# Carried HGRN states loaded ahead into weight buffers, prompt-state stores moved behind the weight loads, and another order of the mixer's projection units

## The chip, the cores and the metric

The kernel runs on one core of a Trainium2 chip. The metric is device time in microseconds for one execution, inputs and outputs in HBM. Before is given by three runs, and the profiled execution is a further one.

## The reference, cut to what matters

One step of a decoder trunk of two layers (width 1024) over 256 prompt rows and 32 sample rows (8 sequences of 4 tokens with carried state). Each layer is a half-step FFN, a mixer and a second half-step FFN, with a layer norm after each:

```
x <- LN(alpha*x + 0.5*SwiGLU_1(x))
z  = x @ W_in            # mix_w_in, 1024 x 3584
o  = concat[RWKV-7 (4 heads of 64), HGRN2 (4 heads of 128), chunk-gMLP (4 of 64)] @ W_out   # mix_w_out
x <- LN(alpha*x + o)
x <- LN(alpha*x + 0.5*SwiGLU_2(x))
```

HGRN2 is a gated linear recurrence. For a sample sequence the output of a head is the query times the carried state (128 x 128, one for each of 8 sequences and 4 heads, 2 MB a layer) plus products within the four new tokens, and the new state is the old one times the total decay plus keys times values. The prompt starts from a zero state. The chunk-gMLP normalises its v half, mixes it over 128 positions, and multiplies by its u half. Everything is float32. Outputs are the trunk's rows, all final states, and the normalised v rows of the samples (`cm_v_sample`).

## The kernel before, in words

All activations stay in SBUF with the features on partitions and the 288 rows along the free dimension. A dense product is done in blocks of at most 512 x 256 weights. `prep` (L338) loads a block on SP's queue into a `raw` buffer (3 of them); ACT rounds it into `wh` and DVE writes the rest into `wl` (3 buffers each), and TensorE makes three products per 128 x 128 piece (`d<-x,wl`, `d<-x,wh` twice), 24 a block. The mixer's input projection for the HGRN and chunk-gMLP parts is made in ten units of 256 columns straight from `raw` in float32 (`d<-ax,raw`, 16 products a unit). `ORDER` (L1798) lists these units: f, q, v, o are forget gate, query, value and output gate of the HGRN (two units each), cv and cu the two halves of the gMLP.

The mixer of a layer is written as generators, one per piece of work (`CHAINS`), which `go` in `mix` (L1695) advances in turn between the units. `hg_scan` builds the HGRN decay products, `hg_mix` makes the prompt's HGRN output, `hg_sample` (L1497) the samples' output and `hg_states` the samples' new states, `cm_mix` (L1624) the gMLP, `rw_prompt` and its fellows the RWKV part. A scheduler of the language then places the instructions on the engines by priorities; each engine executes its list strictly in that order. So an instruction that must wait holds back all that stands behind it on its engine, DMA issues included: SP's list holds nearly all of them.

Names that matter below. `hs` are the four tiles of carried HGRN states of a layer (one a head, 512 KB); `hqm` the masked queries; `hp` their 32 products with the states on TensorE; `hs<-hs,hgP` on POOL the decay of a state, which overwrites the tile that `hp` reads; `hvb` the masked values, `hn` their product with the keys, `hs<-hs,hn` on DVE the sum that is stored as the new state. `cvn` is the gMLP's v and `cst` its statistics, `cO`/`cOs` the mix over positions on TensorE, `cM` its result times u. `hO`, `hS`, `hon`, `hot`, `ho` are the prompt's HGRN output on its way to the layout of `mix_w_out`'s input, `OM`, `gst`, `pgt`, `OT` the same for RWKV, and `x` the split input of `mix_w_out`. That dense product starts with four blocks for output columns 0 to 511 (96 products), whose first group of rows is features 0, 1, 6, 7: RWKV's two and the gMLP's two. PSUM has four banks (`pm`) for all small products.

In the kernel before, the states are loaded in `hg_sample` into tiles of the general pool `m4` (19 buffers), the prompt's new states are stored at the end of `rw_prompt` and `hg_mix`, and all these DMAs stand on SP's queue among the loads of `mix_w_out`.

Of the kernel before, what the change touches and what calls it, by code (L numbers as in the profile page):

```python
# [8 lines left out]
F32 = mybir.dt.float32  # L9
# [11 lines left out]
NS = 32  # L21
# [17 lines left out]
class Trunk:  # L39
# [298 lines left out]
    def prep(self, spec):  # L338

        name, l, ks, n0, pool = spec  # L340
        nk = len(ks)
        nc = self.nc
        raw = self.wp.tile([128, 4, 256], F32, tag="raw", name=f"raw{nc.next_id()}", bufs=B["raw"])
        runs = [i for i in range(nk + 1) if i in (0, nk) or ks[i] != ks[i - 1] + 1]
        for a, b in zip(runs, runs[1:]):
            src = self.I[name][l][ks[a] * 128:(ks[b - 1] + 1) * 128, n0:n0 + 256]
            nc.sync.dma_start(raw[:, a:b], src.rearrange("(c p) n -> p c n", p=128))
        if pool == "raw":
            return raw
        hi = self.wp.tile([128, 4, 256], F32R, tag="wh", name=f"wh{nc.next_id()}", bufs=B["wh"])  # L350
        lo = self.wp.tile([128, 4, 256], F32R, tag="wl", name=f"wl{nc.next_id()}", bufs=B["wl"])
        with self.prio("prep"):
            self.act(hi[:, :nk], raw[:, :nk])
            self.sub(lo[:, :nk], raw[:, :nk], hi[:, :nk].bitcast(F32), nc.gpsimd if pool else None)
        return hi, lo
# [581 lines left out]
    def rw_prompt(self, l, KR, bh, kh, V, eP, em):  # L937

        nc, O = self.nc, self.O
# [191 lines left out]
        for c in range(2):  # L1131
            self.tr(p[0:64, c * 128:(c + 1) * 128], S[:, c, 3])
        so = self.ep.tile([64, 256], F32, tag="rwSo", name=f"rwSo{l}", bufs=1)
        nc.vector.tensor_copy(so, p[0:64, 0:256])
        nc.sync.dma_start(O["rwkv_state_prompt"][l, 0].rearrange("g v k -> v g k"),
                          so.rearrange("p (g k) -> p g k", g=4))

    def rw_load(self, l):
        nc, I = self.nc, self.I
# [307 lines left out]
    def hg_mix(self, l):  # L1447
# [15 lines left out]
        for j in range(2):  # L1463
# [20 lines left out]
                for h in range(4):  # L1484
                    self.stt(SP[:, h], SP[:, h], P[:, 256 * h + 255:256 * h + 256], p[:, h], ALU.mult, ALU.add)
            yield
        nc.sync.dma_start(O["hgrn_state_prompt"][l, 0].rearrange("h k v -> k h v"), SP)

    def hrms(self, nm, sq, n):
        nc = self.nc  # L1490
        r = self.ep.tile([128, 4], F32, tag="hrm", name=f"hrm{nm}", bufs=2)[:, 0:n]
        nc.vector.tensor_reduce(r, sq, axis=AX.X, op=ALU.add)
        self.act(r, r, AF.Sqrt, bias=self.eps[:, 2:3], scale=1.0 / 128)
        nc.vector.reciprocal(r, r)
        return r

    def hg_sample(self, l):  # L1497
        nc, I, O = self.nc, self.I, self.O
# [23 lines left out]
        qm = self.m4([128, 4, 8, 32], f"hqm{l}")  # L1522
        for h in range(4):
            self.mul(qm[:, h], self.hsm(Q)[:, h].unsqueeze(1).to_broadcast([128, 8, 32]), self.tb, gp)
        S0 = []
        for h in range(4):
            s0 = self.m4([128, 8, 128], f"hs0{l}{h}")
            S0.append(s0)
            nc.sync.dma_start(s0, I["state_hgrn"][l, :, h].rearrange("b k v -> k b v"))  # L1529

        p = self.ps(f"hp{l}")[:, 0:128]
        for b in range(8):
# [91 lines left out]
    def cm_mix(self, l, cw):  # L1624
# [6 lines left out]
        for j, (o, n) in enumerate(((0, 128), (128, 128), (T, NS))):  # L1631
            p = self.ps(f"cT{l}{j}")
            for c in range(2):
# [15 lines left out]
        v = vn.rearrange("p (j h) d -> p j (h d)", j=3)  # L1649
        self.mul(v, v, gb[:, 0].unsqueeze(1).to_broadcast([128, 3, 256]), gp)  # L1650
        self.add(v, v, gb[:, 1].unsqueeze(1).to_broadcast([128, 3, 256]), gp)
        nc.sync.dma_start(O["cm_v_sample"][l].rearrange("b t d -> (b t) d"),
                          vn[0:NS, 8:12].rearrange("p h d -> p (h d)"))
        yield
        M = self.a2(f"cM{l}")
        for j in range(2):
# [38 lines left out]
    def mix(self, l, q, x, st):  # L1695
# [51 lines left out]
        def post(f):  # L1747
# [2 lines left out]
            return f(l, q, rw["o"], *self.rwv[6:], lambda: mt(0))  # L1750

        self.rw_load(l)
        ch = {
            "pre": (pre,),
            "prompt": (lambda: self.rw_prompt(l, *rw["v"]), "pre"),
# [16 lines left out]
            self.split(m[0][6 + c], m[1][6 + c], self.cmo[:, c])  # L1772
        r = self.post(("mix_w_out", l), m, KC, 1.0, q["ln"][1], SHIFT[1], GROUPS[E["mo"]])
        go(*[(chain(n, *ch[n]), f, n) for n, f in CHAINS if n in LATE])
        return r


# [17 lines left out]

PLO = {'z': ()}

ORDER = ('f1', 'q0', 'f0', 'q1', 'cu', 'v1', 'cv', 'v0', 'o1', 'o0')  # L1798
SHIFT = (True, True, True)

_INS = ["x_prompt", "x_sample", "state_rwkv", "state_rwkv_shift", "state_hgrn", "ffn1_w_in", "ffn1_w_out",
# [31 lines left out]
```

## Time and profile before

| | us |
|---|---|
| median of 3 runs | 1356.68 (1355.81 to 1357.77) |
| profiled execution | 1356.73 |
| its span in the trace | 1355.0 |
| TensorE busy | 1310.4 (97%) |
| VectorE, ScalarE, GpSimd busy | 908.0, 622.6, 226.3 |

The span is what the trace covers; 1.7 us lie around it. The mixer of layer 0 lies between about 225 and 470 us of the span, that of layer 1 some 660 us later with the same instructions. Matmuls overlap in the records: the time from one to the next is its cost, not the length of one. A product of float32 has two records.

### The profile page before, as it was taken

To read this page: it belongs to the slowest core of one execution; us is meant where nothing else is said; L and a number is where in the kernel's file an instruction comes from. 1 tells how busy PE (TensorE), PEld (TensorE's weight loads), DVE (VectorE), ACT (ScalarE), POOL (GpSimd) and SP (SyncE) were. 2 spreads that over 40 slices of the span, in tenths; PEclk is the share of its full clock that TensorE was granted. 3 is DMA by queue.
4 is the path that set the end of the run, shared out by engine and by line. 5 is a ranking of instruction groups with operands and counts; after the bars stand their busy time and mean duration, and the time that the engine had idled before them with its cause. 6 is when DMAs were issued, how large, how long until landed. Compare 5 with 4: busy or idle time off the path is not lost.

```text
span 1355.0 us, 26724 instructions
## 1 busy us (share of the span) xinstructions
PE 1310.4 (97%) x10842; PEld 1222.9 (90%) x10842; DVE 908.0 (67%) x1704; ACT 622.6 (46%) x1014; POOL 226.3 (17%) x361
## 2 busy tenths in 40 slices
PE   8999999999987999999999999999999789999998
PEld 6999999867867899999999999997777589999997
DVE  3555447865447898774698785597753589977643
ACT  5454435743154464443464443367322546544433
POOL 9200001324343100000100000032452411000002
PEclk9999999999997999999999999999999989999998
DMA  5655555421344655555555554553122554555551
GB/s 179 189 159 169 163 160 162 134 85 49 80 132 116 189 161 162 166 161 163 158 163 164 165 163 156 171 161 99 48 79 79 158 162 142 157 169 159 178 162 52
DMA packets 208154, 194.05 MB, mean 143 GB/s; under 512 B 15912, under 2 KB 206364, under 8 KB 208031
## 3 DMA queue, kind: packets, MB, share of 16 engines
q1 hardware_dynamic: 207326, 190.91, 46.1%
q8 instruction: 85, 1.39, 0.4%
q0 software_dynamic: 608, 1.31, 0.4%
q14 instruction: 39, 0.31, 0.1%
q10 hardware_dynamic: 96, 0.13, 0.0%
HBM read 185.10 MB, written 7.22 MB: 142 GB/s over the span
## 4 chain that ended last, share of the span: by engine, by line
PE 85%; DVE 7%; DMA 3%; issue 3%; ACT 1%; SPq 1%; POOL 1%; POOLq 0%; ACTq 0%; DVEq 0%
PE d L97 74%; DMA hs<-in_state_hgrn 1%; PE hA L97 1%; DVE wl L65 1%; PE pX L97 1%; DMA raw<-in_mix_w_out 1%; DVE x L65 1%; ACT wh L62 1%; PE pE L97 1%; PE pD L97 1%; DVE ax L65 1%; DMA raw<-in_ffn_w_in 1%; DVE zs L77 0%; SPq L1529 0%; DVE OT L65 0%
## 5 line engine op out<-in xcount | busy, mean ns | idle before, releaser
L97 PE MATMUL d<-x,wh 128*128 128x290 f32 (+1 forms) x3328 | 680.3, 299 | 3.9 <-DVE x L65 2.1
L97 PEld LDWEIGHTS d<-x,wh 128*128 128x128 f32 x3328 | 542.2, 190 | 8.1 <-DVE x L77 3.6
L65 DVE TENSOR_TENSOR wl<-raw,wh 128x1024 fp32r<-128x1024 f32 (+1 forms) x304 | 366.2, 1204 | 255.0 <-ACT wh L62 254.0
L62 ACT ACTIVATE wh<-raw 128x1024 fp32r<-128x1024 f32 (+1 forms) x304 | 315.1, 1036 | 422.9 <-PE d L97 268.9
L97 PE MATMUL d<-x,wl 128*128 128x290 f32 (+1 forms) x1664 | 497.6, 299 | 6.9 <-ACT x L62 4.2
L97 PEld LDWEIGHTS d<-x,wl 128*128 128x128 f32 x1664 | 316.3, 190 | 8.8 <-ACT x L62 7.2
L97 PE MATMUL d<-h,wh 128*128 128x288 f32 x1408 | 282.1, 296 | 0.0
L97 PEld LDWEIGHTS d<-h,wh 128*128 128x128 f32 x1408 | 226.2, 188 | 0.2
L97 PE MATMUL d<-h,wl 128*128 128x288 f32 x704 | 207.9, 295 | 0.0
L97 PE MATMUL d<-ax,raw 128*128 128x288 f32 x640 | 174.3, 415 | 0.0
L65 POOL TENSOR_TENSOR lnv<-lnq,lnq 128x288 f32<-128x288 f32 x6 | 8.2, 1375 | 851.0 <-ACT lnq L62 851.0
L97 PEld LDWEIGHTS d<-ax,raw 128*128 128x128 f32 x640 | 115.3, 190 | 30.4 <-issue 2.3
L97 PEld LDWEIGHTS d<-h,wl 128*128 128x128 f32 x704 | 132.5, 188 | 0.2
L62 ACT ACT_TABLE_LOAD x39 | 50.0, 1283 | 1.5 <-PEq L1821 0.8
L62 ACT ACTIVATE h<-sg 128x288 fp32r<-128x288 f32 x88 | 38.1, 435 | 24.2 <-DVE sg L65 20.7
L62 ACT ACTIVATE sg<-yg,ccg 128x288 f32<-128x288 f32 x66 | 34.4, 528 | 30.0 <-DVE yg L77 29.9
L65 DVE TENSOR_TENSOR h<-sg,h 128x288 fp32r<-128x288 f32 x88 | 39.7, 453 | 5.6 <-ACT h L62 5.6
L77 DVE SCALAR_TENSOR_TENSOR ax<-d,ax 128x288 f32<-128x288 f32 x48 | 21.5, 452 | 29.1 <-PE d L97 29.1
L77 DVE SCALAR_TENSOR_TENSOR yu<-nu,ccu,yu 128x288 f32<-128x288 f32 x66 | 34.0, 515 | 0.8
L77 DVE SCALAR_TENSOR_TENSOR yg<-nu,ccg,yg 128x288 f32<-128x288 f32 x66 | 33.9, 516 | 0.8
L62 ACT ACTIVATE lnq<-ax 128x288 f32<-128x288 f32 x48 | 20.9, 436 | 28.6 <-DVE ax L77 28.4
L77 DVE SCALAR_TENSOR_TENSOR sg<-yu,ccu,sg 128x288 f32<-128x288 f32 x66 | 33.4, 510 | 0.0
(481 smaller groups left out, 1271.6 us busy)
## 6 DMA issues: line engine op xcount, KB each, us to landing
raw<-in_ffn_w_in SPq DMA_DIRECT2D x176, 512.0 KB
raw<-in_ffn_w_out SPq DMA_DIRECT2D x80, 512.0 KB
raw<-in_mix_w_in SPq DMA_DIRECT2D x56, 512.0 KB
raw<-in_mix_w_out SPq DMA_DIRECT2D x12, 512.0 KB
raw<-in_ffn_w_out SPq DMA_DIRECT2D x16, 256.0 KB
hs<-in_state_hgrn SPq DMA_DIRECT2D x8, 512.0 KB
out_hgrn_state_sample<-hs SPq DMA_DIRECT2D x8, 512.0 KB
raw<-in_mix_w_out SPq DMA_DIRECT2D x8, 256.0 KB
```

Of the source, the lines that this page charges most:

```text
L62: self.nc.scalar.activation(out, in_, func, **kw)
L65: (eng or self.nc.vector).tensor_tensor(out, a, b, op=op)
L77: self.nc.vector.scalar_tensor_tensor(out, a, s, b, op0=op0, op1=op1)
L97: self.nc.tensor.matmul(out, lhsT, rhs, start=start, stop=stop)
```

## The change

Four things. `hg_load` (new) loads the four state tiles at the start of the mixer, behind the last weight load already issued, into two buffers of `wh` and two of `wl`, which lie idle while the units run from `raw`. The stores of the prompt's states are kept in a list and put on SP's queue behind the last weight load that the mixer issued. `cm_v_sample` is stored from GpSimd's queue. And `ORDER` puts both value units ahead of both gMLP units.

```
--- before.py
+++ after.py
@@ -344,7 +344,7 @@
         runs = [i for i in range(nk + 1) if i in (0, nk) or ks[i] != ks[i - 1] + 1]
         for a, b in zip(runs, runs[1:]):
             src = self.I[name][l][ks[a] * 128:(ks[b - 1] + 1) * 128, n0:n0 + 256]
-            nc.sync.dma_start(raw[:, a:b], src.rearrange("(c p) n -> p c n", p=128))
+            self.lastraw = nc.sync.dma_start(raw[:, a:b], src.rearrange("(c p) n -> p c n", p=128))
         if pool == "raw":
             return raw
         hi = self.wp.tile([128, 4, 256], F32R, tag="wh", name=f"wh{nc.next_id()}", bufs=B["wh"])
@@ -1132,8 +1132,8 @@
             self.tr(p[0:64, c * 128:(c + 1) * 128], S[:, c, 3])
         so = self.ep.tile([64, 256], F32, tag="rwSo", name=f"rwSo{l}", bufs=1)
         nc.vector.tensor_copy(so, p[0:64, 0:256])
-        nc.sync.dma_start(O["rwkv_state_prompt"][l, 0].rearrange("g v k -> v g k"),
-                          so.rearrange("p (g k) -> p g k", g=4))
+        self.late.append((O["rwkv_state_prompt"][l, 0].rearrange("g v k -> v g k"),
+                          so.rearrange("p (g k) -> p g k", g=4)))
 
     def rw_load(self, l):
         nc, I = self.nc, self.I
@@ -1484,7 +1484,7 @@
                 for h in range(4):
                     self.stt(SP[:, h], SP[:, h], P[:, 256 * h + 255:256 * h + 256], p[:, h], ALU.mult, ALU.add)
             yield
-        nc.sync.dma_start(O["hgrn_state_prompt"][l, 0].rearrange("h k v -> k h v"), SP)
+        self.late.append((O["hgrn_state_prompt"][l, 0].rearrange("h k v -> k h v"), SP))
 
     def hrms(self, nm, sq, n):
         nc = self.nc
@@ -1493,6 +1493,15 @@
         self.act(r, r, AF.Sqrt, bias=self.eps[:, 2:3], scale=1.0 / 128)
         nc.vector.reciprocal(r, r)
         return r
+
+    def hg_load(self, l):
+
+        self.hs0 = []
+        with self.tc.issue_after(self.lastraw.ins if hasattr(self.lastraw, "ins") else self.lastraw):
+            for h in range(4):
+                s0 = self.wp.tile([128, 8, 128], F32, tag=("wh", "wl")[h % 2], name=f"hs0{l}{h}", bufs=3)
+                self.nc.sync.dma_start(s0, self.I["state_hgrn"][l, :, h].rearrange("b k v -> k b v"))
+                self.hs0.append(s0)
 
     def hg_sample(self, l):
         nc, I, O = self.nc, self.I, self.O
@@ -1522,11 +1531,7 @@
         qm = self.m4([128, 4, 8, 32], f"hqm{l}")
         for h in range(4):
             self.mul(qm[:, h], self.hsm(Q)[:, h].unsqueeze(1).to_broadcast([128, 8, 32]), self.tb, gp)
-        S0 = []
-        for h in range(4):
-            s0 = self.m4([128, 8, 128], f"hs0{l}{h}")
-            S0.append(s0)
-            nc.sync.dma_start(s0, I["state_hgrn"][l, :, h].rearrange("b k v -> k b v"))
+        S0 = self.hs0
 
         p = self.ps(f"hp{l}")[:, 0:128]
         for b in range(8):
@@ -1649,8 +1654,8 @@
         v = vn.rearrange("p (j h) d -> p j (h d)", j=3)
         self.mul(v, v, gb[:, 0].unsqueeze(1).to_broadcast([128, 3, 256]), gp)
         self.add(v, v, gb[:, 1].unsqueeze(1).to_broadcast([128, 3, 256]), gp)
-        nc.sync.dma_start(O["cm_v_sample"][l].rearrange("b t d -> (b t) d"),
-                          vn[0:NS, 8:12].rearrange("p h d -> p (h d)"))
+        gp.dma_start(O["cm_v_sample"][l].rearrange("b t d -> (b t) d"),
+                     vn[0:NS, 8:12].rearrange("p h d -> p (h d)"))
         yield
         M = self.a2(f"cM{l}")
         for j in range(2):
@@ -1750,6 +1755,8 @@
             return f(l, q, rw["o"], *self.rwv[6:], lambda: mt(0))
 
         self.rw_load(l)
+        self.hg_load(l)
+        self.late = []
         ch = {
             "pre": (pre,),
             "prompt": (lambda: self.rw_prompt(l, *rw["v"]), "pre"),
@@ -1772,6 +1779,10 @@
             self.split(m[0][6 + c], m[1][6 + c], self.cmo[:, c])
         r = self.post(("mix_w_out", l), m, KC, 1.0, q["ln"][1], SHIFT[1], GROUPS[E["mo"]])
         go(*[(chain(n, *ch[n]), f, n) for n, f in CHAINS if n in LATE])
+
+        with self.tc.issue_after(self.lastraw.ins if hasattr(self.lastraw, "ins") else self.lastraw):
+            for dst, src in self.late:
+                self.nc.sync.dma_start(dst, src)
         return r
 
 
@@ -1795,7 +1806,7 @@
 
 PLO = {'z': ()}
 
-ORDER = ('f1', 'q0', 'f0', 'q1', 'cu', 'v1', 'cv', 'v0', 'o1', 'o0')
+ORDER = ('f1', 'q0', 'f0', 'q1', 'v1', 'v0', 'cv', 'cu', 'o1', 'o0')
 SHIFT = (True, True, True)
 
 _INS = ["x_prompt", "x_sample", "state_rwkv", "state_rwkv_shift", "state_hgrn", "ffn1_w_in", "ffn1_w_out",
```

Where it moves instructions, in layer 0 (layer 1 has the same order):

POOL at the end of the mixer, before: `cvn` is the gMLP's normalisation, `hs` the decay of the states.

```order
L1630 MEMSET cvn_4668 128x256
L1512 COPY r_4769<-hgK_4036 128x384
L65 TENSOR_TENSOR cvn_4668<-cvn_4668,cst_4693 128x768 x2
L65 TENSOR_TENSOR cvn_4668<-cvn_4668,cgb_3426 128x768 x2
L1620 DMA cgb_11470<-in_cm_ln_g 128x256
L1621 DMA cgb_11470<-in_cm_ln_b 128x256
L1512 COPY r_4819<-hgV_4426 128x384
L65 TENSOR_TENSOR cM_4790<-cM_4790,ccu_4218 128x576
L1618 DMA cbs_11465<-in_cm_bs 64x128 x4
L65 TENSOR_TENSOR hqm_4852<-hgQ_3583,tb 128x256 x4
L65 TENSOR_TENSOR hs_4857<-hs_4857,hgP_3506 128x1024
L65 TENSOR_TENSOR hs_4863<-hs_4863,hgP_3506 128x1024
```

The gMLP was through with POOL before the first state was touched; the other two states and two `hvb` follow. The same place in the change:

```order
L65 TENSOR_TENSOR cvn_4781<-cvn_4781,cst_4828 128x768
L65 TENSOR_TENSOR hs_3438<-hs_3438,hgP_3514 128x1024
L65 TENSOR_TENSOR hs_3440<-hs_3440,hgP_3514 128x1024
L65 TENSOR_TENSOR hs_3444<-hs_3444,hgP_3514 128x1024
L65 TENSOR_TENSOR hs_3442<-hs_3442,hgP_3514 128x1024
L1376 MEMSET hAS_12099 128x128
L65 TENSOR_TENSOR hvb_4950<-hk_4453,mb 96x1024
L65 TENSOR_TENSOR cvn_4781<-cvn_4781,cst_4828 128x768
L65 TENSOR_TENSOR cvn_4781<-cvn_4781,cgb_3426 128x768 x2
L1657 DMA out_cm_v_sample<-cvn_4781 32x256
L1625 DMA cgb_11470<-in_cm_ln_g 128x256
L1626 DMA cgb_11470<-in_cm_ln_b 128x256
```

The four decays and one `hvb` now stand between the first step of the normalisation and its other three; `cM` follows, then the last `hvb`.

TensorE in the change, around the last product of the last unit (`d_4878<-ax,raw_4880`):

```order
L97 MATMUL hp_4567<-hs_3438,hqm_4562 32x128
L97 MATMUL d_4878<-ax,raw_4880 128x288
L97 MATMUL hp_4567<-hs_3440,hqm_4562 32x128
L97 MATMUL hp_4567<-hs_3442,hqm_4562 32x128
L97 MATMUL hp_4567<-hs_3444,hqm_4562 32x128
L97 MATMUL hp_4567<-hvs_4449,hAS_4047 128x128
L97 MATMUL pO_4930<-rwS_4627,QP_4626 64x64 x6
L97 MATMUL pO_4931<-rwS_4627,QP_4626 64x64 x6
L97 MATMUL hS_4955<-hVT_4668,hKT_4669 128x128 x4
L97 MATMUL cO_4974<-cwt_3407,cvn_4781 64x128 x4
L97 MATMUL cO_4980<-cwt_3407,cvn_4781 64x128 x4
L97 MATMUL cOs_4986<-cwsm_3416,cvn_4781 64x32 x4
```

The last reads of the states end with the units, where before they came some 14 us after them; and `cO`, which stood among the last unit's products, now stands behind them all.

ACT in the change, in the same stretch (`wh_5176` is the second weight block of `mix_w_out`, in a buffer that held state `hs_3438`):

```order
L62 ACTIVATE hsqs_4807<-hp_4567 128x128
L62 ACT_TABLE_LOAD
L62 ACTIVATE qs_4863<-d_4773 128x288
L62 ACTIVATE qs_4870<-d_4775 128x288
L62 ACTIVATE qs_4863<-qs_4863,pv_1120 128x288
L62 ACTIVATE qs_4870<-qs_4870,pv_1120 128x288
L62 ACTIVATE csq_4829<-cvn_4781 128x768
L62 ACT_TABLE_LOAD
L62 ACTIVATE hrm_4917<-hrm_4917,eps 128x4
L62 ACTIVATE wh_5176<-raw_5172 128x1024
L62 ACTIVATE cst_4828<-cst_4828,eps 128x12
L62 ACTIVATE hSP_4908<-hS_4955 128x512
```

The square and the root of the gMLP's statistics (`csq`, `cst`) stand behind the square of `hp`, and the root also behind `wh_5176`, which may only be written when the store of state `hs_3438` has landed.

## Rows read from the trace of the kernel before

**Rows 1.** The page's 40 slices (busy tenths; granted TensorE clock; DMA).
```profile
PE   8999999999987999999999999999999789999998
PEclk9999999999997999999999999999999989999998
DMA  5655555421344655555555554553122554555551
```

**Rows 2.** The chain that ended last, both mixers: start, length (us), what.
```profile
401.18 0.99 PE d L97 x4
403.77 2.02 SPq L1529
405.84 8.34 DMA hs<-in_state_hgrn
414.31 2.33 PE hp L97 x60
433.13 1.06 PE d L97 x8
443.57 5.82 DMA raw<-in_mix_w_out
501.86 159.27 PE d L97 x1190
1065.79 8.43 DMA hs<-in_state_hgrn
```

**Rows 3.** TensorE's timeline, layer 0: idle time before an instruction in brackets.
```profile
407.73 0.61 PE L97 MATMUL hp<-hs,hqm 128*32 128x128 f32 x2 [4.71 <-POOL hqm L65]
422.92 0.61 PE L97 MATMUL d<-x,wl 128*128 128x288 f32 x1 [2.10 <-ACT x L62]
429.32 1.09 PE L101 MATMUL hot<-ident,hon 128*128 128x128 f32 x4 [1.95 <-DVE hon L65]
436.10 0.40 PE L97 MATMUL hn<-hvb,hk 96*128 96x512 f32 x1
436.34 0.43 PE L97 MATMUL d<-x,wh 128*128 128x288 f32 x2
453.68 0.72 PE L97 MATMUL lnm<-lns,ones 128*128 128x288 f32 x2 [1.74 <-DVE lns L65]
```

**Rows 4.** Windows of 2 us, layer 0: busy by engine, granted clock, DMA share, GB/s.
```profile
428.00:430.00 2.00, 0.68 (x4) 0.71 (x5) 1.87 (x4) 0.00 (x0) 0.26 (x1) 0.50 0.00 0
432.00:434.00 2.00, 2.00 (x13) 1.87 (x13) 1.63 (x7) 2.00 (x9) 0.00 (x0) 0.90 0.00 0
```

**Rows 5.** POOL's timeline, layer 0.
```profile
375.73 1.47 POOL L65 TENSOR_TENSOR cvn<-cvn,cst 128x768 f32<-128x768 f32 x1 [4.41 <-DVE cst L1640]
382.71 3.70 POOL L65 TENSOR_TENSOR cvn<-cvn,cgb 128x768 f32<-128x768 f32 x2
400.73 2.32 POOL L65 TENSOR_TENSOR cM<-cM,ccu 128x576 f32<-128x576 f32 x1 [12.40 <-DVE cM L65]
416.12 8.07 POOL L65 TENSOR_TENSOR hs<-hs,hgP 128x1024 f32<-128x1024 f32 x4 [8.45 <-PE hp L97]
424.30 3.96 POOL L65 TENSOR_TENSOR hvb<-hk,mb 96x1024 fp32r<-96x1024 f32 x2
```

**Rows 6.** DVE's timeline, layer 0: the same operation under POOL's work and after it.
```profile
418.80 1.57 DVE L65 TENSOR_TENSOR x<-OT,x 128x256 fp32r<-128x256 f32 x1
429.47 0.41 DVE L65 TENSOR_TENSOR x<-OT,x 128x256 fp32r<-128x256 f32 x1
```

**Rows 7.** Groups by shape, 396 to 436 us: count, busy us, mean ns, idle before.
```profile
L62 ACT ACTIVATE hvb<-hk,mb 96x128 fp32r<-96x128 f32 x16 | 4.9, 387 | 0.0
L65 DVE TENSOR_TENSOR wl<-raw,wh 128x1024 fp32r<-128x1024 f32 x3 | 4.1, 1371 | 8.6 <-ACT wh L62 8.6
L65 DVE TENSOR_TENSOR hs<-hs,hn 128x512 f32<-128x512 f32 x3 | 1.9, 679 | 0.0
L97 PE MATMUL cO<-cwt,cvn 128*64 128x128 f32 x16 | 1.1, 279 | 0.0
```

More of the change, by code (lines that the diff above doesn't have):

```diff
@@ L346, in prep @@
             src = self.I[name][l][ks[a] * 128:(ks[b - 1] + 1) * 128, n0:n0 + 256]
-            nc.sync.dma_start(raw[:, a:b], src.rearrange("(c p) n -> p c n", p=128))
+            self.lastraw = nc.sync.dma_start(raw[:, a:b], src.rearrange("(c p) n -> p c n", p=128))
         if pool == "raw":
@@ L1134, in rw_prompt @@
         nc.vector.tensor_copy(so, p[0:64, 0:256])
-        nc.sync.dma_start(O["rwkv_state_prompt"][l, 0].rearrange("g v k -> v g k"),
-                          so.rearrange("p (g k) -> p g k", g=4))
+        self.late.append((O["rwkv_state_prompt"][l, 0].rearrange("g v k -> v g k"),
+                          so.rearrange("p (g k) -> p g k", g=4)))
     def rw_load(self, l):
@@ L1486, in hg_mix @@
             yield
-        nc.sync.dma_start(O["hgrn_state_prompt"][l, 0].rearrange("h k v -> k h v"), SP)
+        self.late.append((O["hgrn_state_prompt"][l, 0].rearrange("h k v -> k h v"), SP))
     def hrms(self, nm, sq, n):
@@ L1495, in hrms, with hg_load @@
         return r
+    def hg_load(self, l):
+        self.hs0 = []
+        with self.tc.issue_after(self.lastraw.ins if hasattr(self.lastraw, "ins") else self.lastraw):
+            for h in range(4):
+                s0 = self.wp.tile([128, 8, 128], F32, tag=("wh", "wl")[h % 2], name=f"hs0{l}{h}", bufs=3)
+                self.nc.sync.dma_start(s0, self.I["state_hgrn"][l, :, h].rearrange("b k v -> k b v"))
+                self.hs0.append(s0)
     def hg_sample(self, l):
@@ L1524, in hg_sample @@
             self.mul(qm[:, h], self.hsm(Q)[:, h].unsqueeze(1).to_broadcast([128, 8, 32]), self.tb, gp)
[L1525 to L1529, printed above, removed]
+        S0 = self.hs0
         p = self.ps(f"hp{l}")[:, 0:128]
@@ L1651, in cm_mix @@
         self.add(v, v, gb[:, 1].unsqueeze(1).to_broadcast([128, 3, 256]), gp)
-        nc.sync.dma_start(O["cm_v_sample"][l].rearrange("b t d -> (b t) d"),
-                          vn[0:NS, 8:12].rearrange("p h d -> p (h d)"))
+        gp.dma_start(O["cm_v_sample"][l].rearrange("b t d -> (b t) d"),
+                     vn[0:NS, 8:12].rearrange("p h d -> p (h d)"))
         yield
@@ L1752, in mix @@
         self.rw_load(l)
+        self.hg_load(l)
+        self.late = []
         ch = {
@@ L1774, in mix @@
         go(*[(chain(n, *ch[n]), f, n) for n, f in CHAINS if n in LATE])
+        with self.tc.issue_after(self.lastraw.ins if hasattr(self.lastraw, "ins") else self.lastraw):
+            for dst, src in self.late:
+                self.nc.sync.dma_start(dst, src)
         return r
@@ L1796 @@
 PLO = {'z': ()}
-ORDER = ('f1', 'q0', 'f0', 'q1', 'cu', 'v1', 'cv', 'v0', 'o1', 'o0')
+ORDER = ('f1', 'q0', 'f0', 'q1', 'v1', 'v0', 'cv', 'cu', 'o1', 'o0')
 SHIFT = (True, True, True)
```

## Prediction

> **What bounds it now.** I read the page's slices first, then the chain of waits, and then the timelines of the engines around the place where the chain leaves TensorE. TensorE is busy in nine tenths of nearly every slice; the exceptions inside the program are slices 12 and 13 and, a layer later, 33 [rows 1]. So a change is worth something only there, at the end of each mixer, or where it opens a new hole. In that stretch the chain goes from the last product of a projection unit, which ends at 401.18 + 0.99 = 402.2, to SP's queue (2.02), the transfer of a carried state (8.34), the query-times-state products `hp` (2.33), and it is back on the dense product of `mix_w_out` at 433.1 [rows 2]. Layer 1 shows the same transfer with 8.43. TensorE idles in several pieces: 4.71, 2.10, 1.95 and, at the layer norm, 1.74 [rows 3]. Meanwhile its granted clock is 0.50, the lower level of 1.2 GHz, and by 432 to 434 it is 0.90 on average [rows 4].
>
> So there is a real wait for the states, some 10 us on the chain. But other work fills most of it, and what follows (`hp`, POOL's decay, the HGRN output, the split of the input) is needed anyway. The question is what the last late thing will be once the states are there.
>
> **Early loads.** Four DMAs of 512 KB are issued near the mixer's start, at some 250 to 270 us of the span. The DMA digits of the seventh to tenth slices (203 to 339 us) are 5, 4, 2 and 1 [rows 1], and the `wh`/`wl` buffers are unused there. I take zero; the bound is +5 a layer, should a unit's weights queue behind them, priced by the last dense weight transfer on the chain, 5.82 [rows 2].
>
> **Prompt-state stores and the gMLP's store.** Nothing on the chip waits for a store except a buffer's next user. Behind the last weight load they delay no weights. I take zero for their own part, and for the gMLP's store on POOL, which stands after the arithmetic that matters.
>
> **Units.** The same products run, in another order, and TensorE has enough of them. `hp` now stands among the last ones, which puts 2.33 ahead of the units' end: 402.2 + 2.3 = 404.5 for the last read of a state. What else moves ahead (transposes, first `hn`) and behind (`cO`, `cOs`, `pO`, `hS`) is a few microseconds each way; I count it as nothing, with ±2.
>
> **POOL.** Here I see the cost. Before, POOL has done all of the gMLP's normalisation at 375.7 to 386.4 (a step of 1.47, the last two 3.70) and `cM` at 400.7, while the decays of the states come at 416.1, after `hp` [rows 5]. In the change the four decays and one `hvb` stand between the first normalisation step and the others. The decays overwrite the tiles that `hp` reads, so POOL stops until 404.5. Then: decays 8.07, a memset 0.2, `hvb` 3.96/2 = 2.0 [rows 5], which makes 414.7; then the three normalisation steps, 1.47 + 3.70, which makes 419.9. TensorE has the position mix `cO` of 1.1 us [rows 7] behind that, and only `pO` and `hS` before it: about 14 us idle. With `cOs` and the sum on VectorE I put the start of POOL's `cM` at 421.8, its end (2.32) [rows 5] at 424.1. The gMLP supplies features 6 and 7, in the first group of rows of `mix_w_out`, and their split on ScalarE waits for `cM`.
>
> The root of the gMLP's statistics stands on ScalarE behind the second weight split, which writes a buffer that held a state and hence waits for that state's store: first decay plus two additions of 0.68 [rows 7] put its issue at 404.5 + 2.0 + 1.4 = 407.9, the landing, at 5.82 as for a weight transfer [rows 2], at 413.7, and the root some 1.5 later, about when POOL comes to need it. At 8.34, as a state's load [rows 2], it costs +2 to +3.
>
> **From there to the dense product.** Behind that split, ScalarE and VectorE carry in order what before was done while they waited for states: eight `hvb` scalings (4.9/2 = 2.5), a weight split (1.4), four state additions (4 x 0.68 = 2.7) [rows 7], the transposes `hot` (1.1) [rows 3] and four steps of the output norm at some 0.7, the mean of the 128x512 form [rows 7], and about 17 small operations of RWKV's output and the input's split at 0.41 [rows 6], 7.0: together 2.5 + 1.4 + 2.7 + 1.1 + 2.8 + 7.0 = 17.5. RWKV's `OT` stands last, and features 0 and 1 come from it. The dense product then begins at 424.1 + 17.5 = 441.6. If the engines share this work instead of passing it on, the least I can make of it is 12.
>
> Before, it went on at 433.1 [rows 2], by which time some 20 of its products had run, at 159.27/1190 = 0.134 each [rows 2], 2.7; seven `hn`, a start every 0.24 [rows 3], 1.7, were still to come. An unbroken start would have been at 433.1 - 2.7 + 1.7 = 432.1. **Lateness: 9.5 a layer.**
>
> **Clock.** Before, TensorE is at 0.50 until it has been working again for some microseconds: from 429.3 to about 433.8 [rows 3, 4]. In the change the longer holes fall at the same level, and the dense product itself pays for the recovery: 4.5 us at half speed lose 2.2 (bounds 0 and 3).
>
> **Layer norm.** The wait of 1.74 at `lnm` [rows 3] has some nine products between now, -1.2 (bound -1.7).
>
> Sum: 9.5 + 2.2 - 1.2 = 10.5 a layer, 21 for both. The sum stands against the profiled execution, 1356.73 with a span of 1355.0; the median, 1356.68, is the same within a tenth. 1356.7 + 21 = **1378**.
>
> The Trainium skill ("SBUF — State Buffer", section "Who interferes with whom") says that a VectorE instruction with two SBUF inputs and a GpSimd instruction reading SBUF exclude each other entirely. The trace agrees: the same split of `x` takes 1.57 under POOL's decays and 0.41 after them [rows 6]. By the order in the change the splits run after the decays, and the sum takes 0.41; by the page they would cost 1.57 if POOL's last `hvb` or the `cM` step still ran beside four of them, 4 x 1.16 = +4.6 a layer, some 1387.
>
> **Bounds.** Low: 12 for 17.5, units -2, clock 0, layer norm -1.7: 9.5 - 5.5 - 2 - 1.7 = +0.3 a layer, 1357. High: 10.5 with the store's +3, splits slowed +4.6, clock +0.8: some +19 a layer, 1394. All of that together with a late load I leave out.
>
> **Rivals.** *Faster, the wait is simply gone.* 2.02 + 8.34 = 10.4 a layer leave the chain [rows 2], and the chain from the last `hp` to the dense product stays what it was, 433.1 - (414.3 + 2.3) = 16.5: 404.5 + 16.5 is 421, eleven earlier, and twice 10.4 gives 1336. For it: the state transfer and queue are plainly on the chain in both layers. Against: in those 16.5 us before, POOL had only the decays and two `hvb`, with the gMLP finished. It decides at 432.1 - 404.5 = 27.6: if that chain is shorter, the change is not slower; I count 37.
>
> The Trainium skill ("DMA: Bandwidth & Descriptors", section "Rules for kernel authors") advises issuing a DMA early and waiting late so that its fixed cost overlaps; the wait of 8.34 agrees that there is something to overlap, and by this rule alone the rival holds.
>
> *Slower still, the stores.* If a state's store lands as late as its load, 8.34 [rows 2], and both `wh` and `wl` splits stand in order behind it, the norm and RWKV's tail wait together, +5.6 a layer: about 1389.
>
> *About as before.* The tail after `cM` is half of what I count, since ScalarE, VectorE and TensorE pass it along while POOL works: 8 to 9 us less a layer, 1355 to 1364.
>
> **How the numbers follow.** Forecast (1357 to 1394 on its own): 0.65. Wait gone: 0.18, between 1336 and 1354. Stores: 0.08. About as before: 0.09. A measurement of this kernel can tell about 0.2% from no change, 1354.0 to 1359.4. Slower: 0.63 of the forecast, 0.08, and 0.04 of the fourth case, 0.75; no change 0.07; faster 0.18. The range runs from 1350 to 1394, which leaves out most of the wait-gone case.
>
> **What would show it.** No wait for a state transfer on TensorE or in the chain. POOL's `cvn` steps after the decays, at some 415 to 420 of the span. TensorE idle for some 14 us waiting for POOL's `cvn` at `cO`. The first `mix_w_out` product at about 441, under a clock of 0.50. ScalarE's second weight split waiting for a store of a state. The prediction is wrong if that first product comes before 432, or if a unit waits for its weights near 270.

## The result, and the profile after

The change takes 1398.88 us (1398.32 to 1399.86) against 1356.24 for the kernel before in the same comparison: ratio 1.0313, interval 1.0297 to 1.0330. That is 42.6 us slower, twice the 21 forecast, and outside the range. The profiled execution's span is 1396.5 instead of 1355.0.

The page's slices of the kernel after (busy tenths of TensorE, then its granted clock); they answer to [rows 1].

```profile
PE   8999999999994999999999999999999679999998
PEclk9999999999995999999999999999999779999999
```

The holes are where they were, at the end of each mixer, and deeper: in layer 0 one slice with 4 where two had 8 and 7, in layer 1 6 and 7 instead of 7 and 8. The first product of the layer norm behind the mixer (`lnm`) shows how much each layer loses. TensorE's timeline after, both layers, and the one of layer 1 before:

```profile
474.52 0.72 PE L97 MATMUL lnm<-lns,ones 128*128 128x288 f32 x2
1156.48 0.72 PE L97 MATMUL lnm<-lns,ones 128*128 128x288 f32 x2
```

```profile
1114.03 0.72 PE L97 MATMUL lnm<-lns,ones 128*128 128x288 f32 x2 [0.96 <-DVE lns L65]
```

Before, the first came at 453.68 [rows 3]: 20.8 later after one layer, 42.5 after two. The `lnm` ahead of the first mixer comes at the same time in both kernels (213.6 and 213.8), so the loss lies between the mixer's start and the end of its dense product. There, in layer 0, the chain of waits of the kernel after reads (start, length, what):

```profile
411.88 1.00 POOL hs L65
413.75 5.65 POOL hs L65 x3
...
422.23 1.79 POOL cvn L65
...
427.83 1.98 PE cO L97 x16
...
433.57 2.84 DVE x L65 x2
...
448.35 2.48 DVE hs L65 x4
...
452.45 22.12 PE d L97 x153
```

No state transfer is left in it, where [rows 2] had 8.34. In its place stand GpSimd's decays and normalisation, then VectorE. TensorE's own waits in the mixer, 225 to 495 (after; total, times, longest):

```profile
PE cO L97 <- POOL cvn L65: 9.5, 1, 9.5
PE hot L101 <- DVE hon L65: 4.3, 1, 4.3
PE pgt L101 <- DVE OM L65: 3.9, 1, 3.9
PE d L97 <- ACT x L62: 1.9, 1, 1.9
PE cwp L101 <- DMA cws<-in_cm_ws: 1.0, 1, 1.0
```

Windows of the kernel after (busy by engine, granted clock, DMA share, GB/s), for [rows 4]:

```profile
411.00:428.00 17.00, 6.13 (x48) 4.37 (x49) 9.40 (x23) 11.46 (x19) 14.90 (x9) 0.62 0.27 82
428.00:452.00 24.00, 13.45 (x69) 10.82 (x69) 18.25 (x38) 7.34 (x26) 7.04 (x9) 0.57 0.30 77
452.00:456.00 4.00, 3.54 (x15) 3.55 (x16) 2.20 (x4) 1.80 (x3) 0.00 (x0) 0.51 0.57 169
456.00:460.00 4.00, 4.00 (x32) 4.00 (x32) 1.30 (x2) 1.06 (x1) 0.00 (x0) 1.00 0.42 137
```

TensorE works 6.1 of 17 and 13.5 of 24 us, at a mean granted clock of 0.62 and 0.57, little over its lower level of 0.50, and the dense product's first four microseconds still run at 0.51. GpSimd's timeline after, for [rows 5]:

```profile
390.29 1.47 POOL L65 TENSOR_TENSOR cvn<-cvn,cst 128x768 f32<-128x768 f32 x1 [16.92 <-DVE cst L1645]
411.88 7.52 POOL L65 TENSOR_TENSOR hs<-hs,hgP 128x1024 f32<-128x1024 f32 x4 [20.12 <-PE hp L97]
...
422.23 1.79 POOL L65 TENSOR_TENSOR cvn<-cvn,cst 128x768 f32<-128x768 f32 x1 [0.83 <-DVE cst L1651]
424.10 3.68 POOL L65 TENSOR_TENSOR cvn<-cvn,cgb 128x768 f32<-128x768 f32 x2
```

Between the first step of the normalisation and the second lie 32 us, 20.1 of them a wait for `hp` to be done with the first state. That is the row forecast, with about its lengths, but 7.4 us later: 411.9, not 404.5. What ScalarE does meanwhile turned out to matter as much; its timeline after:

```profile
413.29 0.28 ACT L62 ACTIVATE hsqs<-hp 128x128 f32<-128x128 f32 x1 [6.64 <-PE hp L97]
...
416.32 0.84 ACT L62 ACTIVATE csq<-cvn 128x768 f32<-128x768 f32 x1
...
419.62 0.29 ACT L62 ACTIVATE cst<-cst,eps 128x12 f32<-128x12 f32 x1
```

The square of `hp` stands ahead of the gMLP's square `csq` and waits for the last `hp` as well, and the root is through at 419.9. GpSimd's idle 0.83 before 422.23 is a wait for what follows from it, VectorE's reciprocal at 421.94.

### The profile page after: what moved, and what is told of

It reads as the page before. It is cut to its first block, busy times and chain, and to the rows that moved or that the text cites. A ratio compares the mean times of both kernels' runs of the same rounds, so it can differ in the third digit from the quotient of the medians.

```text
span 1396.5 us, 26677 instructions
## 1 busy us (share of the span) xinstructions
PE 1331.7 (95%) x10842; PEld 1232.4 (88%) x10842; DVE 899.1 (64%) x1704; ACT 619.4 (44%) x1012; POOL 227.4 (16%) x363
## 4 chain that ended last, share of the span: by engine, by line
PE 86%; DVE 6%; POOL 3%; issue 2%; DMA 1%; ACT 1%; SPq 0%; POOLq 0%; DVEq 0%; ACTq 0%
PE d L97 75%; PE hA L97 1%; PE pX L97 1%; POOL hs L65 1%; DMA cws<-in_cm_ws 1%; POOL cvn L65 1%; DVE wl L65 1%; PE hp L97 1%; PE pE L97 1%; PE pD L97 1%; DMA raw<-in_ffn_w_in 0%; DVE hs L65 0%; PE hT L101 0%; DVE x L65 0%; ACT wh L62 0%
## 5 line engine op out<-in xcount | busy, mean ns | idle before, releaser
L77 DVE SCALAR_TENSOR_TENSOR yg<-nu,ccg,yg 128x288 f32<-128x288 f32 x66 | 33.9, 516 | 0.8
```

Source lines behind the costliest of these rows:

```text
L77: self.nc.vector.scalar_tensor_tensor(out, a, s, b, op0=op0, op1=op1)
```

## Experiments: which part of the change

Four runs, each against the kernel before on the same chip. That kernel's medians lay between 1354.7 and 1356.2 in the comparisons of this document, so a difference between two runs from different comparisons is good to one or two us.

**The old order of units** (the change otherwise whole):

```
-ORDER = ('f1', 'q0', 'f0', 'q1', 'v1', 'v0', 'cv', 'cu', 'o1', 'o0')
+ORDER = ('f1', 'q0', 'f0', 'q1', 'cu', 'v1', 'cv', 'v0', 'o1', 'o0')
```

> The change with the order of units of before; the early loads, the late stores and the gMLP's store on GpSimd stay. Theory (the order of the units is the whole loss: it puts the decays ahead of the gMLP's normalisation on GpSimd and spreads hp among the unit's products): 1336 to 1357, most likely 1345, from hp starting at about 408 of the span without waiting for a transfer, 6.6 a layer earlier than before, less 0.75 a layer for the gMLP's weights that land later behind the states. GpSimd's cvn steps end ahead of the decays, as before. Rival (the states in the split buffers are the loss: splits of mix_w_out wait for the stores of states): 1385 to 1399, with ScalarE's split waiting for a store for 8 or more a layer.

Measured 1356.11, ratio 1.0011 (1.0002 to 1.0021). The loss is gone, as the theory had it, but the expected gain of 11 is not there.

**The new order alone**, on the kernel before (the same line, the other way).

> The kernel before with only the new order of units. Theory (the order is the loss): 1395 to 1415: the same row of decays ahead of the normalisation on GpSimd, hp in pieces among the products, and up to 8 a layer more where hp waits for its states. Rival (only the states in the split buffers, or both together, lose): 1350 to 1362.

Measured 1389.52, ratio 1.0249 (1.0233 to 1.0264). The order makes some 34 of the 42 by itself, less than the theory's 1395 to 1415; the states' own wait did not come on top of it, since `hp` starts at 372 of the span there.

**The early loads alone**, on the kernel before with its order; `hg_load` is as in the change:

```
+        self.hg_load(l)
-            s0 = self.m4([128, 8, 128], f"hs0{l}{h}")
-            nc.sync.dma_start(s0, I["state_hgrn"][l, :, h].rearrange("b k v -> k b v"))
+        S0 = self.hs0
```

> The kernel before with only the early loads into the split buffers; order of units, prompt-state stores and the gMLP's store as before. Theory: within 5 of the run with the old order of units, so 1340 to 1357, since the deferred stores have nothing on the chain behind them. Rival (the deferred stores give what the early loads cannot, because SP's queue is blocked by the prompt state's store until 434 of the span): 1354 to 1362 here, and 10 or more below that with the stores deferred.

Measured 1356.12, ratio 1.0004 (0.9994 to 1.0015): the same as with the late stores. Those are worth nothing here, in either direction.

**Order and early loads, stores as before**: the edits of the two runs above together, to divide the remaining 9 us.

> The kernel before with the early loads and the new order of units; prompt-state stores and the gMLP's store as before. The new order alone took 1389.5, the whole change 1398.9. Theory (the early loads make the 9 us between them: the gMLP's weights land later, and buffers of the splits wait for the states' stores): 1395 to 1400. Rival (the late stores make it): 1386 to 1392.

Measured 1399.01, ratio 1.0318 (1.0304 to 1.0331). So the 9 us between the order alone and the whole change are the early loads', not the stores'. About 1 us a layer of it is seen: the gMLP's small weights `cws` land in 5.9 instead of 4.0 us beside the states, and TensorE waits 1.1 for them (not at all with the order alone). The rest was not taken apart; from `lnm` to `lnm` around the mixer, both layers lose: 262.6 and 260.0 here, 258.5 and 254.9 with the order alone.

## Experiments: where the expected gain of the early states went

In the old order with early states, the bulk of `hp` runs at 406.7 to 408.6 in layer 0, more than 7 us earlier than in [rows 2], and yet the time stays. VectorE's timeline of that run (the old order of units), with GpSimd's beside it:

```profile
410.77 5.76 DVE L65 TENSOR_TENSOR OT<-OT,G 128x256 f32<-128x256 f32 x1
417.24 1.32 DVE L65 TENSOR_TENSOR x<-OT,x 128x256 fp32r<-128x256 f32 x1
418.49 2.11 DVE L65 TENSOR_TENSOR OT<-OT,G 128x256 f32<-128x256 f32 x1
```

```profile
408.71 7.52 POOL L65 TENSOR_TENSOR hs<-hs,hgP 128x1024 f32<-128x1024 f32 x4
```

RWKV's gate product `OT`, with both inputs in SBUF, takes 5.76: it ends as the four decays end, at 416.2 to 416.5. Before, the decays started so late, behind the states, that the first `OT` ran beside the first of them and took 0.82. The wait for the transfer has become a wait for the decays.

That holds for layer 0 alone. VectorE's, GpSimd's and TensorE's timelines of the same run:

```profile
1073.55 1.82 DVE L65 TENSOR_TENSOR OT<-OT,G 128x256 f32<-128x256 f32 x1
```

```profile
1071.30 7.89 POOL L65 TENSOR_TENSOR hs<-hs,hgP 128x1024 f32<-128x1024 f32 x4 [1.87 <-PE hp L97]
```

```profile
458.88 0.72 PE L97 MATMUL lnm<-lns,ones 128*128 128x288 f32 x2
...
1114.48 0.72 PE L97 MATMUL lnm<-lns,ones 128*128 128x288 f32 x2
```

In layer 1 the same product takes 1.82, as it gets its turn after the second decay. Layer 0 reaches `lnm` 5.2 later than before, layer 1 only 0.5 later, so what layer 0 loses is won back behind it, most of it in layer 1's mixer (235.4 from `lnm` to `lnm`, before 238.7; layer 0's is 244.9, before 239.9). The unchanged time is a loss and a gain, not nothing twice. The run with the early loads alone shows the same pair, 5.77 and 1.82. Why the two layers differ was not tested. A test takes the decays off GpSimd.

**Old order, decays on VectorE**: fused into the additions, 32 small ones a layer in place of eight.

```
-'hs': (0, 1, 2, 3)
+'hs': ()
```

> The change with the order of units of before, where the early loads gave nothing (1356.1), and with the decays fused into the additions on VectorE (32 small ones a layer in place of eight) instead of four on GpSimd. Theory (the gain of the early states is lost in VectorE's gate product OT, 5.7 in place of 0.3 while GpSimd decays the states): OT falls to 0.3 to 0.5, the dense product starts 4 to 8 earlier in each layer, less the longer additions, of some 4: 1340 to 1352. Rival (VectorE is full there and the blocked instruction only moves its work): 1354 to 1366.

Measured 1348.79, ratio 0.9957 (0.9941 to 0.9972): a little faster than both kernels. The same products of layer 0 in its VectorE timeline:

```profile
410.27 0.70 DVE L65 TENSOR_TENSOR OT<-OT,G 128x256 f32<-128x256 f32 x1
...
412.93 0.41 DVE L65 TENSOR_TENSOR OT<-OT,G 128x256 f32<-128x256 f32 x1
```

5.76 is 0.70, 2.11 is 0.41, and the dense product starts at 411.5 instead of 417.0. Part of the gain is the clock: TensorE waited 5.3 for that start with the decays on GpSimd and 0.25 here, and its granted clock was 0.50 from 416 to 426 there and 1.00 from 411 to 424 here. The early states were worth something, once nothing took their place.

**The same edit (`'hs': ()`) on the kernel before**, without early loads.

> The kernel before with nothing but the decays fused into the additions on VectorE, as in the run at 1348.8 that also has the early loads. Theory (early loads and unblocked VectorE are each worth little alone, since the state wait covers OT and OT takes the place of the state wait): hp still waits for its states until about 414 of the span, and only the x split of 1.6 and the second OT of 2.1 come down to some 0.4 each: 1350 to 1357. Rival (the decays on GpSimd are the whole cost and the loads nothing): 1346 to 1350.

Measured 1354.91, ratio 0.9999 (0.9986 to 1.0012). Neither part alone changes the time (early loads 1.0004, decays 0.9999); the two together give 0.9957. In layer 0 that is what two waits side by side look like: its mixer takes 239.9 before, 242.7 and 241.1 with one part, 237.1 with both. In layer 1 the loads alone give more than half of it: 238.7, 236.0 and 237.8, 234.0.

**Old order with the samples' HGRN chain at a raised priority**, so that `hp` and the decays run under the units: with the decays on GpSimd, all on VectorE, and two on each.

```
-'hsam': -150
+'hsam': 300
```

> The change with the order of units of before and with the samples' HGRN chain at the raised priority: hp in one piece among the units, two decays ahead of cM on GpSimd and two behind. Theory (with the states there early, hp and the decays can be done under the units' products, so that neither the state wait of before nor VectorE's block at OT is left): 1334 to 1350. Rival (something else at the mixer's end holds the dense product, as the split or the layer norm): 1353 to 1360.

> The change with the order of units of before, the decays fused on VectorE, and the samples' HGRN chain at the raised priority (hp in one piece among the units). Theory (both parts of the lost gain at once): hp off the stretch behind the units and no block of VectorE: 1338 to 1347. Rival (with hp early, VectorE's 32 fused additions and its other work are the bound, so the earlier hp gives nothing more): 1347 to 1353.

> The same, but with two of the four decays on GpSimd (ahead of cM, under the units' products) and two fused on VectorE. Theory (GpSimd is idle under the units and VectorE is the scarce one behind them): 2 to 4 less than with all decays fused: 1336 to 1346. Rival (cM comes 3.8 later behind the two decays and holds features 6 and 7): 1348 to 1358.

Measured: 1352.76, ratio 0.9985 (0.9971 to 1.0000); 1358.28, 1.0025 (1.0009 to 1.0041); 1351.38, 0.9975 (0.9959 to 0.9991). The third is a little faster than before and the first at the edge of its interval, both less than hoped; the second misses even its rival. In its chain a split of `mix_w_out` waits 3.75 for a state's store (`DMA out_hgrn_state_sample`), which with all decays on VectorE comes late. So the price of states in the split buffers, which the prediction's second rival named, is real where VectorE is late.

**The loads among the units**: the run at 1348.79 with `hg_load` called when the HGRN scan starts.

```
-        self.hg_load(l)
+        def scan():
+            self.hg_load(l)
+            yield from self.hg_scan(l)
```

> The run at 1348.8 (old order of units, decays on VectorE), with the four state loads put among the loads of the units, behind the tenth, in place of the mixer's start, so that the gMLP's small weights no longer share the DMA engines with them. Theory (the wait for those weights, 0.9 a layer, is the early loads' only cost in the old order): 1345 to 1349. Rival (here the state loads delay a unit's weights): 1350 to 1358.

Measured 1350.77, ratio 0.9968 (0.9956 to 0.9980), against 0.9957 with overlapping intervals: no difference is shown, and the gain of 1 to 2 us is not there either.

## Experiments: what holds the mixer in the new order

**Decays behind the normalisation** on GpSimd.

```
-"hst": (lambda: self.hg_states(l), "hsam"),
+"hst": (lambda: self.hg_states(l), "hsam", "cm"),
```

> The change, with the four decays behind the gMLP's four normalisation steps on GpSimd (the generator of the new states starts when that of the gMLP is through); order of units as in the change. Theory (GpSimd's row is what holds cO and with it the dense product): cO starts within 3 of the last product of the units, the wait of TensorE for cvn of 9.5 goes, and 8 to 14 a layer come off: 1370 to 1383; the interleaved hp stays. Rival (VectorE's and ScalarE's tail behind cM is the bound, whichever comes first on GpSimd): under 4 a layer, 1391 to 1399.

Measured 1385.16, ratio 1.0219 (1.0202 to 1.0237): 6.9 a layer back, less than the theory said. `cO` starts at 410.4, 17 earlier, and TensorE now waits 10.9 for `hos`, ScalarE's scaled `hp`. The edit moved more than it names: ScalarE's `csq` stands ahead of the square of `hp` in this run (391.5, not 416.3), so two holds of the normalisation went at once.

**`hp` first**: the raised priority as above, in the new order; and **`hp` in runs**, the priority lowered:

```
-'hsam': -150
+'hsam': -600
```

> The change, with the priority of the samples' HGRN chain raised, so that hp runs as one piece of 33 products some 30 products of the units earlier and the four decays are done on GpSimd ahead of the whole normalisation. Theory (the loss is GpSimd's normalisation waiting behind decays that wait for the last hp, plus hp in pieces): TensorE's wait for cvn falls below 2 a layer (9.5 in the change), hp costs 2.3 to 3 instead of 6.1, so 13 to 22 a layer come off, 1355 to 1372. Rival (what ends last is the tail of VectorE and ScalarE behind cM, 24.6 from cO to the dense product in the change, whatever comes before): under 8 a layer, above 1383.

> The change with the priority of the samples' HGRN chain lowered: hp in two pieces of 25 and 8 products in place of some fifteen, the decays still ahead of the normalisation on GpSimd. Theory (pieces of hp among the units' products cost TensorE 6.1 in place of 2.3): hp costs 2.3 to 3, the last hp comes 3 to 4 earlier a layer at least, 1384 to 1393. Rival (hp costs 6 there whatever its pieces, as it reads from two parts of memory): 1396 to 1401.

Measured 1362.39, ratio 1.0056 (1.0041 to 1.0071), and 1372.25, ratio 1.0130 (1.0114 to 1.0147). These are the largest steps: some 36 and 27 of the 42.6 come back, the second well past its theory (1384 to 1393), as its last `hp` comes 20 us earlier and not 3 to 4. TensorE's timelines of the two, and of the change for comparison:

```profile
365.80 1.95 PE L97 MATMUL hp<-hs,hqm 128*32 128x128 f32 x64
...
412.08 1.09 PE L97 MATMUL cO<-cwt,cvn 128*64 128x128 f32 x16
```

```profile
385.69 1.50 PE L97 MATMUL hp<-hs,hqm 128*32 128x128 f32 x18 [2.43 <-DVE hAT L94]
...
392.72 0.64 PE L97 MATMUL hp<-hs,hqm 128*32 128x128 f32 x14
...
418.54 1.09 PE L97 MATMUL cO<-cwt,cvn 128*64 128x128 f32 x16 [1.85 <-POOL cvn L65]
```

```profile
396.47 0.41 PE L97 MATMUL hp<-hs,hqm 128*32 128x128 f32 x2
396.81 0.75 PE L97 MATMUL d<-ax,raw 128*128 128x288 f32 x2
...
427.83 1.98 PE L97 MATMUL cO<-cwt,cvn 128*64 128x128 f32 x16 [9.55 <-POOL cvn L65]
```

With the last `hp` at 368 or 393 instead of 413, `cO` follows the units' products within 2 us, and the wait of 9.5 is gone or 1.9. The products of `hp` cost 1.9 and 3.1 against 6.1, near what was expected, but that is 3 to 4 us a layer; the rest is what waits behind the last one.

**Decays on VectorE in the new order**, `hp` in pieces as in the change.

> The change with its own order of units and hp in pieces as in the change; only the decays are fused into the additions on VectorE. GpSimd then has no instruction ahead of the normalisation that waits for hp. Theory (GpSimd's row is the largest part of the loss, hp in pieces the smaller): TensorE's wait for cvn at cO falls from 9.5 to below 3, 14 to 22 of the 42 come back: 1376 to 1385. Rival (the wait at cO only moves the time at which the same tail of some 22 to 25 from cO to the dense product begins, and this tail is the loss, while the longer additions on VectorE lengthen it): 1386 to 1399.

Measured 1400.34, ratio 1.0326 (1.0311 to 1.0341). The theory that GpSimd's row is the largest part falls. ScalarE's, GpSimd's and TensorE's timelines of this run say why:

```profile
416.65 0.28 ACT L62 ACTIVATE hsqs<-hp 128x128 f32<-128x128 f32 x1 [1.52 <-PE hp L97]
...
420.64 0.84 ACT L62 ACTIVATE csq<-cvn 128x768 f32<-128x768 f32 x1
...
422.99 0.29 ACT L62 ACTIVATE cst<-cst,eps 128x12 f32<-128x12 f32 x1
```

```profile
424.24 1.47 POOL L65 TENSOR_TENSOR cvn<-cvn,cst 128x768 f32<-128x768 f32 x1 [5.29 <-DVE cst L1651]
```

```profile
429.52 1.97 PE L97 MATMUL cO<-cwt,cvn 128*64 128x128 f32 x16 [12.91 <-POOL cvn L65]
```

GpSimd has no decay left and is idle, yet the normalisation is later still: it waits for the statistics, which stand behind the square of `hp` on ScalarE. Two lists hold it, and both hang on the last `hp`. The decays on VectorE also have a price of their own here: a weight split on ScalarE waits 7.17 for the store of a state (0.35 in the change), and TensorE 4.9 for the split of `x` behind it.

**Statistics first**: the samples' chain is held at the square of `hp` until the root of the gMLP's statistics is through; once on the change (the decays then fall behind the normalisation too), once with the decays on VectorE.

```
+        while f"cmr{l}" not in self.done:
+            yield False
         self.act(sq, p, AF.Square)
```

> The change, with the samples' chain held at the square of hp until the gMLP's statistics are through, so that on ScalarE csq and the root of cst stand ahead of that square, and on GpSimd the normalisation ahead of the decays; hp itself stays in pieces among the units. Theory (in the change ScalarE's square of hp and GpSimd's decays each hold the normalisation until the last hp, so that taking away the one alone, as with the decays on VectorE, gives nothing): TensorE's wait for cvn at cO goes (9.5), the dense product starts 8 to 13 a layer earlier: 1373 to 1384. Rival (the tail from cO to the dense product grows by what cO gains): 1390 to 1399.

> The same hold, with the decays fused on VectorE as in the run at 1400.3. It differs from that run only in ScalarE's order. Theory: the wait of 12.9 for cvn goes, 8 to 13 a layer come off the 1400.3: 1374 to 1385. Rival (the position of the statistics on ScalarE does not matter): 1395 to 1402.

Measured 1389.06, ratio 1.0253 (1.0232 to 1.0274), and 1394.20, ratio 1.0288 (1.0266 to 1.0309). In both the wait for `cvn` at `cO` is gone and `cO` starts at 413.7 and 413.6, so ScalarE's square was the second hold. But only 9.8 and 6.1 us come back where 16 or more were expected. Most of what `cO` gains is lost behind it, as the first run's rival said: from `cO` to the dense product it takes 33.2 and 37.0, where it was 24.6 and 24.1. `hp` itself ends later, its last product (with `hvs`) at 419.9 and not 412.8, since `cO` now stands among its pieces; and at the end ScalarE waits 3.98, in the second run 8.70, for the store of a state (ScalarE and TensorE of the first run):

```profile
420.34 0.28 ACT L62 ACTIVATE hsqs<-hp 128x128 f32<-128x128 f32 x1 [8.99 <-PE hp L97]
...
445.47 1.06 ACT L62 ACTIVATE wh<-raw 128x1024 fp32r<-128x1024 f32 x1 [3.98 <-DMA out_hgrn_state_sample<-hs]
```

```profile
424.90 0.79 PE L97 MATMUL hn<-hvb,hk 96*128 96x512 f32 x1 [4.60 <-ACT hvb L62]
...
446.88 0.61 PE L97 MATMUL d<-x,wl 128*128 128x288 f32 x1 [5.01 <-ACT x L62]
```

**`hp` first and decays on VectorE** in the new order (`'hsam': 300` and `'hs': ()`).

> The change with its own order of units, the samples' HGRN chain at the raised priority and the decays fused on VectorE, so that GpSimd does the normalisation as soon as its statistics are there. Theory (the order loses through GpSimd's row and hp in pieces alone): 1346 to 1356, near the old order's 1348.8. Rival (values first also delays the gMLP itself, whose chain from cv to cM then ends behind the units): 1357 to 1366, no better than the 1362.4 with hp first alone.

Measured 1368.23, ratio 1.0101 (1.0073 to 1.0129): slower than `hp` first alone, and 2 past the upper end of its rival. From `cO` at 410.3 to the dense product at 435.5 it is 25 us, though every product with the states was done by 367. One part is the order: `cO`, the end of the chain that starts with `cv`, comes at 388 to 402 in the kernels with the old order and at 410 or later in those with the new one, whatever the HGRN does. Another is the buffers. From this run's chain of waits and its ScalarE timeline:

```profile
418.69 3.21 DMA out_hgrn_state_sample<-hs
...
430.76 3.20 DMA out_hgrn_state_sample<-hs
```

```profile
434.07 1.06 ACT L62 ACTIVATE wh<-raw 128x1024 fp32r<-128x1024 f32 x1 [6.91 <-DMA out_hgrn_state_sample<-hs]
```

Two stores of states stand on the chain between `cO` and the dense product. The split that waits 6.91 holds the split of RWKV's output behind it, for which the dense product waits 4.9. With the decays on GpSimd and `hp` first, that split waits 0.34. No run put the early states into buffers of their own, so what the sharing costs in all is not shown.

## Why the prediction came out half right

The direction and the place were right: slower, at the end of both mixers, with TensorE waiting for GpSimd's `cvn` at `cO` (9.5, not 14), no transfer on the chain, and the dense product restarting at the lower clock level. One sign did not come: ScalarE's second weight split, at 418.7, waited for no store. The size was half. Term by term, in layer 0:

- **The step that failed first: "Units".** It put the last read of a state at 404.5 and counted the pieces that move across the units' end as nothing. Measured, the last read ends at 412.8, 8.3 later, and the decays, which need only the first state to be free, at 411.9, 7.4 later. Added up from the trace (start to next start, waits apart), `hp` cost 6.1, not 2.3 as in the one piece of [rows 2], since the new order scatters it in sixteen pieces: 3.8. The gMLP's late weights hold TensorE for 1.0. What moved ahead (transposes, `hO`, `hn`) costs 4.3 and what moved behind 2.5: 1.7, within the ±2. The other 2 or so are mainly small products, RWKV's above all, that stayed ahead and cost more in their new places. The order of TensorE's list showed the pieces of `hp`; I priced them by a run.
- **GpSimd's stretch**, 15.4 by the sum, took 15.9 from the decays to `cO`. The size was right and the reason half of it: I took ScalarE's root for ready "about when POOL comes to need it" and priced it as a small upper bound. It was a second hold of about the same length, as the run without decays on GpSimd shows, where TensorE waited 12.9.
- **From `cO` to the dense product**, 21.7 by the sum, took 24.6. Two things on the chain were longer than the sum had them: one split of `x` took 2.78 for 0.41, beside GpSimd's DMA issue and last `hvb`, as [rows 6] had shown for one (1.57) and as the bound had it; and `cO`, at a granted clock of 0.50, took 1.98 for 1.1. The rest of this term, waits for `hon` (4.3), `OM` (3.9) and `x` (1.9) in series, was priced in one lump and not taken apart.
- **Clock**: the first 24 products of the dense product took 4.8 us (452.5 to 457.3) in place of 24 x 0.134 = 3.2, so 1.6 was lost, not 2.2. [rows 4] says as much of before: 0.90 over 432 to 434 is 0.4 us at the lower level, so that stretch ended at 432.4, not 433.8, and half of 3.1 us is 1.6. The wait at `lnm` is gone, as forecast. Together: 22.1 from the dense product to `lnm`, where the sum's unbroken start gives 453.7 - 432.1 = 21.6, so 0.5 was added and not 1.0.

7.4 + 0.5 + 2.9 - 0.5 = 10.3, and with the 10.5 forecast that is the 20.8 measured. Nearly three quarters of the miss is the first term. The range's upper end did not cover it: it gave "Units" only ±2.

Early loads at nothing was within its bounds but not zero: about 1 a layer for the gMLP's weights in either order, and some 9 us in all in the new order, most of it unexplained. Late stores at nothing was right (1356.11 against 1356.12 in the old order, 1398.88 against 1399.01 in the new).

The rival "the wait is simply gone" fails for a reason that I had not seen. Even with the old order the wait's end gave nothing in sum, since in layer 0 GpSimd's decays then fall on VectorE's `OT`. The Trainium skill ("SBUF — State Buffer", section "Who interferes with whom") has the rule, that the two exclude each other for a whole instruction; the prediction cited it for the splits of `x` at 1.57. The runs agree with it where `OT` took 0.82 to 2.13, one decay at a time; the 5.76 in layer 0 of the old order is three decays in a row. I weighed it for the instruction that it slowed before, and not for the one that would stand beside the decays once they move. The rival of the stores decided nothing in the change itself (ScalarE's split waits 0.35 there, behind the start of the dense product), but it is real in other kernels of the new order: where the decays are on VectorE, or behind the gMLP, that split waits 2.7 to 8.7 for a store, just ahead of the dense product.

Open: how the remaining 7 us or so of the early loads in the new order come about, why early loads lose in layer 0 and win in layer 1 of the old order, and why `cO` to the dense product takes 21.6 to 25.1 in every kernel whose `cO` comes behind the units, however early `hp` is. The stores are not all of it: with the order alone, where no split waits for them, it is 22.4.

## What to carry to other kernels

Before removing a wait, list what ran under it on the other engines and put each next to its new neighbours: here a transfer of 8.3 us covered a conflict of 5.8 in one of two layers, and only both edits together gave a gain (0.9957). Look at each layer by itself: an unchanged total hid a loss of 5 and a gain of nearly as much. When an order table moves a product, price it as it will stand in the list, piece by piece, and look for every in-order list whose next instruction reads its last piece: freeing one such list gave nothing (1.0326 against 1.0313), freeing both 10 to 14 of 42 us, and making that last piece early some 36.

## What the runs showed of the hardware that was not expected

A piece of small float32 products has a price of its own, whether it is one product or three. In the run with `hp` first, 64 records (32 products) take 1.89 us, 365.80 to 367.69, 0.06 a product. In the change, a single such product between two products of a unit takes 0.34 to the next start (396.47 to 396.81), over five times as much, and three take 0.35 (410.36 to 410.71). TensorE's timeline of the change:

```profile
410.36 0.42 PE L97 MATMUL hp<-hs,hqm 128*32 128x128 f32 x6
410.71 0.75 PE L97 MATMUL d<-ax,raw 128*128 128x288 f32 x2
```

All 14 pieces of at most three products in the change take 0.34 or 0.35. The products of the units themselves cost nearly the same before and after, 33.3 and 33.9 us from 350 to the units' end. What the 0.34 is made of was not measured.

A VectorE product of two SBUF inputs of 128x256 took 0.4 alone and, in layer 0 of the old order with early states, 5.76 beside four GpSimd products of 128x1024 back to back: it did not get in between them, and the four took 7.52 with and without it. It is not always so. In layer 1 of the same run it took 1.82 and the four 7.89, and in the kernel before such products took 0.82, 1.57 and 2.13, each let in behind one of the four, which then took 8.07. What decides between the two was not found.
